# Four small stores of zeros between the first loads of a mixture-of-experts kernel

## The chip, the cores and the metric

The kernel runs on one core of a Trainium2 chip. The metric is the device time of one execution in microseconds, the median of several runs. One further execution is taken by the hardware profiler; all durations below come from that one.

## What is computed

Eight experts each apply a two-layer network to 256 rows of their own. The reference, cut to what matters:

```
x: (8, 256, 512)   w1: (8, 512, 2048)   w2: (8, 2048, 512)   b1: (8, 2048)   b2: (8, 512)   all float32
h   = maximum(x @ w1 + b1, 0)
out = h @ w2 + b2                       (8, 256, 512) float32
```

Each expert has 4 MB of w1 and 4 MB of w2 in memory, so the weights are 64 MB of reads; x adds 4 MB and the output is 4 MB of writes.

## The kernel before

Everything is cast from float32 to float16 while it is loaded: a load issued from GpSimd (POOL in the profile) reads 4 MB of weights and writes 2 MB into the on-chip memory. All weight loads, the x of experts 2 to 7, and the stores of the results of experts 0 to 6 are issued from GpSimd and form one queue, here called the ring. Only the first two x (L188, float32, cast on VectorE at L201), b1 (L189) and the last expert's stores (L142, L143, L149) go by the queues of SyncE and ScalarE.

For an expert e, first_product (L108) computes h transposed: 16 blocks of 128 hidden units, four matmuls each (L113), and ScalarE adds b1, applies the maximum and writes float16 (L120). In the middle of it, the x of the next expert is transposed on TensorE (L100) and copied out by VectorE (L106). second_product (L151) runs three experts later (LAG = 3): b2 is put into the accumulators by a matmul with ones (L163), then 32 matmuls of 128x512 (L175) add h times w2; VectorE and ScalarE copy one half of the rows each (L138, L139), and flush (L130) issues the store (L132).

The order of the ring is written out by hand. The first w1 (L190) and b2 (L191) come first. Then a list of issues, each with the step from which it may go, is built at L221 to L241: for s from 1 on, the x of expert s (load_x, L69), its w1 (load_w1, L75), the w2 of expert s - 3 (load_w2, L85), and from s = 6 on the store of expert s - 6. The w2 of the last expert comes in eight pieces (load_w2_piece, L91), with the remaining stores between them. The main loop (L243) puts the due issues ahead of each step's matmuls. In the text, x2 is the x of expert 2, w1(3) the w1 of expert 3, and so on; the ring begins w1(0), b2, w1(1), x2, w1(2), x3, w1(3), w2(0), x4, w1(4), w2(1), x5, w1(5), w2(2), x6, w1(6), w2(3), store of expert 0, x7, w1(7), w2(4), store of expert 1, w2(5).

An issue waits for its buffer: there are three for w1, three for w2, four for x, three for the results (L42 to L48). It also waits for a completion semaphore: the compiled program gives the transfers of the ring eight of them in turn, so a transfer is not issued before the one eight places ahead of it has landed. For instance, the first x that waits for that, x5, waits for x2, and the store of expert 0 for w1(4).

Of the kernel before, what the change touches and what calls it, by code (L numbers as in the profile page):

```python
# [11 lines left out]
def kernel(  # L12
# [9 lines left out]
    nc = tc.nc  # L22
    fp32 = mybir.dt.float32
# [3 lines left out]
    P = 128  # L27
# [4 lines left out]
    LAG = 3  # L32
# [5 lines left out]
    def ordered(ins):  # L38
        return tc.keep_in_program_order(ins)

    singles = ctx.enter_context(tc.tile_pool(name="singles", bufs=1))
# [14 lines left out]
    b2_sb = singles.tile([1, E * H], fp16)  # L56
    b1_rows = singles.tile([E * 2, M // 2], fp32)
    b1T = singles.tile([P, nJ, E], fp32)

    x16 = [None] * E  # L60
    xT = [None] * E
# [68 lines left out]
    def flush(e):  # L130
        dst, src = pending.pop(e)
        ordered(nc.gpsimd.dma_start(out=dst, in_=src))  # L132

    def store(e, po, c0, c1, split):
        w = c1 - c0
        pool = out_pool if w == H else singles
        out_sb = pool.tile([P, nTB, w], fp32, tag=f"out{c0}_{w}", name=f"out{w}")
        nc.vector.tensor_copy(out=out_sb[:, 0, :], in_=po[0])  # L138
        nc.scalar.copy(out=out_sb[:, 1, :], in_=po[1])  # L139
        dst = out[e].rearrange("(p tb) h -> p tb h", tb=nTB)[:, :, c0:c1]  # L140
        if split and c1 == H:
            nc.sync.dma_start(out=dst[:, 0, :], in_=out_sb[:, 0, :])  # L142
            nc.scalar.dma_start(out=dst[:, 1, :], in_=out_sb[:, 1, :])  # L143
        elif e in RING:
            pending[e] = (dst, out_sb)
        else:
            step = P // PARTS.get(e, 1)
            for lo in range(0, P, step):
                nc.sync.dma_start(out=dst[lo : lo + step], in_=out_sb[lo : lo + step])  # L149

    def second_product(e):  # L151
# [18 lines left out]
        for lo, hi, p0, p1, t in w2_sb[e]:  # L170
            mine = [b for b in blocks if p0 <= b[0] and b[1] <= p1]
            for tb in range(nTB):
                for j in range(lo, hi):
                    for c0, c1, _, _ in mine:
                        ordered(nc.tensor.matmul(  # L175
                            out=acc[c0, tb],
                            lhsT=hT[e][:, j, tb * P : (tb + 1) * P],
                            rhs=t[:, j - lo, c0 - p0 : c1 - p0],
                            start=False,
                            stop=(j == nJ - 1),  # L180
                        ))
            if hi == nJ:
                for c0, c1, _, _ in mine:
                    store(e, [acc[c0, tb] for tb in range(nTB)], c0, c1, e == E - 1)

    x32 = singles.tile([P, nXF32, nTB, H], fp32)
    for e in range(nXF32):
# [4 lines left out]
        out=b2_sb,  # L192
        in_=b2.rearrange("e h -> (e h)").rearrange("(o f) -> o f", o=1),
    ))
    make_identity(nc, ident)
    make_identity(nc, ident16)
    nc.vector.memset(ones1, 1.0)
# [6 lines left out]
    for j in range(nJ):  # L204
        for s in range(2):
            ordered(nc.tensor.matmul(  # L206
                out=pb[s * 64 : (s + 1) * 64, j, :, :],
# [5 lines left out]
    for s in range(2):  # L213
        nc.vector.tensor_copy(  # L214
            out=b1T[s * 64 : (s + 1) * 64, :, :], in_=pb[s * 64 : (s + 1) * 64, :, :, s]
# [4 lines left out]

    ring = []  # L221
    for s in range(1, E + LAG - 1):
        if s < E:
            if s >= nXF32:
                ring.append((s - 2, load_x, (s,)))
            ring.append((s - 2, load_w1, (s,)))
        if s >= LAG:
            ring.append((s - 2, load_w2, (s - LAG,)))
        if s >= 2 * LAG:
            ring.append((s - 2, flush, (s - 2 * LAG,)))  # L230
# [51 lines left out]
```

## Time and profile before

| what | value |
|---|---|
| median of 4 runs | 183.55 us (183.44 to 183.67) |
| the profiled execution, its own time | 183.32 us |
| its span, from the first instruction to the last | 181.5 us |
| TensorE (PE) busy | 137.6 us, 76% of the span |
| ScalarE (ACT) busy | 62.7 us, 35% |
| GpSimd (POOL) busy, issuing transfers for the most part | 22.1 us, 12% |
| VectorE (DVE) busy | 13.4 us, 7% |
| moved by DMA | 40.58 MB counted at the destination, mean 224 GB/s |
| memory read and written | 71.39 MB and 4.19 MB, 416 GB/s over the span |
| one w1 load, issue to landing, median of 8 | 33.7 us |
| one w2 load of 2048 KB, issue to landing, median of 6 | 45.8 us |
| one store of 512 KB from the ring, issue to landing, median of 7 | 27.8 us |

Issue to landing is the time in the queue and in transfer together: the ring is in order, and a load issued early waits there for those ahead of it. A share of the DMA engines can come out a little over 100% in a short window, because a packet is counted where it starts. In lists of instructions, the text in square brackets is the idle time of the engine just before, and what ended it.

### The profile page before, as it was taken

To read this page: it belongs to the slowest core of one execution; us is meant where nothing else is said; L and a number is where in the kernel's file an instruction comes from. 1 tells how busy PE (TensorE), PEld (TensorE's weight loads), DVE (VectorE), ACT (ScalarE), POOL (GpSimd) and SP (SyncE) were. 2 spreads that over 40 slices of the span, in tenths; PEclk is the share of its full clock that TensorE was granted. 3 is DMA by queue.
4 is the path that set the end of the run, shared out by engine and by line. 5 is a ranking of instruction groups with operands and counts; after the bars stand their busy time and mean duration, and the time that the engine had idled before them with its cause. 6 is when DMAs were issued, how large, how long until landed. Compare 5 with 4: busy or idle time off the path is not lost.

```text
span 181.5 us, 2204 instructions
## 1 busy us (share of the span) xinstructions
PE 137.6 (76%) x946; PEld 98.5 (54%) x946; DVE 13.4 (7%) x22; ACT 62.7 (35%) x138; POOL 22.1 (12%) x46
## 2 busy tenths in 40 slices
PE   0555999579650999749992899709999995999890
PEld 0544889469540845637481755707549642434560
DVE  0320011001000101010100101001010010101010
ACT  0022689647660331806063330803409601010100
POOL 7100011300300010111010000200004003113300
PEclk9999999978996699978999699975999999999999
DMA  5989999999999999999998999999999999999995
GB/s 180 279 191 233 231 209 195 207 252 213 197 231 220 199 217 231 192 216 227 231 220 183 232 231 213 191 285 217 199 224 215 283 195 271 217 238 289 214 278 196
DMA packets 7017, 40.58 MB, mean 224 GB/s; under 512 B 1216, under 2 KB 2256, under 8 KB 4960
## 3 DMA queue, kind: packets, MB, share of 16 engines
q0 software_dynamic: 5872, 38.81, 97.9%
q1 hardware_dynamic: 688, 0.95, 1.5%
q10 hardware_dynamic: 448, 0.69, 1.0%
q8 instruction: 7, 0.11, 0.2%
q14 instruction: 2, 0.02, 0.0%
HBM read 71.39 MB, written 4.19 MB: 416 GB/s over the span
## 4 chain that ended last, share of the span: by engine, by line
DMA 70%; PE 14%; issue 8%; another core or an unknown queue 3%; POOL 2%; ACT 0%; POOLq 0%
DMA x<-in_x_dram 24%; DMA w2sb<-in_w_dram 22%; DMA w1sb<-in_w_dram 13%; DMA w<-in_w_dram 11%; PE acc L175 6%; PE ph L113 6%; PE psx L100 1%; POOL w2sb L85 1%; POOL w1sb L75 1%; POOL out_dram L132 0%; PE acc L163 0%; POOL b_sb L191 0%; POOL ident masks.py:199 0%; POOL ident masks.py:197 0%
## 5 line engine op out<-in xcount | busy, mean ns | idle before, releaser
L113 PE MATMUL ph<-xT,w1sb 128*128 128x256 f16 x512 | 68.2, 299 | 8.7 <-DMA w1sb<-in_w_dram 8.7
L120 ACT ACTIVATE hT<-ph,b1T 128x256 f16<-128x256 f32 x128 | 57.0, 474 | 44.0 <-PE ph L113 43.6
L113 PEld LDWEIGHTS <-w1sb 128*128 128x128 f16 x512 | 61.5, 149 | 14.7 <-DMA w1sb<-in_w_dram 9.6
L175 PE MATMUL acc<-w2sb,hT 128*128 128x512 f16 x224 | 49.5, 379 | 1.9 <-DMA w2sb<-in_w_dram 1.9
L175 PEld LDWEIGHTS <-hT 128*128 128x128 f16 x288 | 27.2, 98 | 32.7 <-issue 6.7
L139 ACT COPY out<-acc 128x512 f32<-128x512 f32 (+2 forms) x9 | 4.9, 541 | 59.6 <-PE acc L175 59.6
L100 PE MATMUL psx<-ident,x 128*128 128x128 f16 x64 | 7.0, 275 | 21.1 <-DMA x<-in_x_dram 20.4
L100 PEld LDWEIGHTS <-x 128*128 128x128 f16 x64 | 5.6, 130 | 22.1 <-DMA x<-in_x_dram 21.3
L75 POOL DMA_DIRECT2D w1sb<-in_w_dram x8 | 4.4, 554 | 60.7 <-PE ph L113 59.9
L106 DVE COPY xT<-psx 128x1024 f16<-128x1024 f16 x8 | 5.5, 692 | 83.3 <-PE psx L100 83.3
L138 DVE COPY out<-acc 128x512 f32<-128x512 f32 (+2 forms) x9 | 5.7, 632 | 71.8 <-PE acc L175 71.8
L85 POOL DMA_DIRECT2D w2sb<-in_w_dram x8 | 4.3, 536 | 49.1 <-PE acc L175 49.1
L206 PE MATMUL pb<-ident,b_rows 16*64 16x16 f32 x64 | 3.7, 265 | 6.7 <-DMA b_rows<-in_b_dram 6.7
L175 PE MATMUL acc<-w,hT 128*128 128x320 f16 (+1 forms) x64 | 7.8, 272 | 1.1 <-DMA w<-in_w_dram 1.1
L206 PEld LDWEIGHTS pb<-ident,b_rows 16*64 16x64 f32 x64 | 3.6, 198 | 6.7 <-issue 6.7
L91 POOL DMA_DIRECT2D w<-in_w_dram x8 | 5.0, 624 | 12.0 <-DMA w2sb<-in_w_dram 9.2
L132 POOL DMA_DIRECT2D out_dram<-out x7 | 3.8, 542 | 21.8 <-ACT out L139 13.1
L120 ACT ACT_TABLE_LOAD x1 | 1.3, 1283 | 11.1 <-DVE b1T L214 11.1
L163 PE MATMUL acc<-b_sb,ones 1*128 1x512 f16 (+2 forms) x18 | 4.8, 355 | 0.0
L69 POOL DMA_DIRECT2D x<-in_x_dram x6 | 3.3, 545 | 5.9 <-DMA w2sb<-in_w_dram 5.4
L163 PEld LDWEIGHTS <-ones 1*128 1x128 f16 x18 | 1.1, 92 | 2.2 <-issue 2.1
L201 DVE CAST x<-x 128x1024 f16<-128x1024 f32 x2 | 1.4, 694 | 4.5 <-DMA x<-in_x_dram 4.4
(9 smaller groups left out, 2.6 us busy)
## 6 DMA issues: line engine op xcount, KB each, us to landing
w1sb<-in_w_dram POOLq DMA_DIRECT2D x8, 2048.0 KB, 33.7
w2sb<-in_w_dram POOLq DMA_DIRECT2D x6, 2048.0 KB, 45.8
out_dram<-out POOLq DMA_DIRECT2D x7, 512.0 KB, 27.8
w2sb<-in_w_dram POOLq DMA_DIRECT2D x2, 1024.0 KB, 24.8
x<-in_x_dram POOLq DMA_DIRECT2D x6, 256.0 KB, 38.8
w<-in_w_dram POOLq DMA_DIRECT2D x2, 384.0 KB, 18.9
x<-in_x_dram ACTq DMA_DIRECT2D x1, 512.0 KB, 5.4
x<-in_x_dram SPq DMA_DIRECT2D x1, 512.0 KB, 4.6
```

The lines of the kernel that those rows point to most:

```text
L75: ordered(nc.gpsimd.dma_start(out=w1_sb[e], in_=w1[e].rearrange("(p kc) m -> p kc m", kc=nKC)))
L85: ordered(nc.gpsimd.dma_start(out=t[:, lo : lo + step, :], in_=src[:, lo : lo + step, :]))
L91: ordered(nc.gpsimd.dma_start(out=t, in_=src[:, lo:hi, c0:c1]))
L100: ordered(nc.tensor.transpose(out=pt[:, kc, tb * P : (tb + 1) * P], in_=x16[e][:, tb, :].rearrange("p (q kc) -> p q kc", kc=nKC)[:, :, kc] ...
L106: nc.vector.tensor_copy(out=xT[e], in_=pt)
L113: ordered(nc.tensor.matmul(out=ph, lhsT=w1_sb[e][:, kc, :].rearrange("p (q j) -> p q j", j=nJ)[:, :, j], rhs=xT[e][:, kc, :], start=(kc == 0),
L120: nc.scalar.activation(out=hT[e][:, j, :], in_=ph, func=mybir.ActivationFunctionType.Relu, bias=b1T[:, j, e : e + 1], scale=1.0,)
L138: nc.vector.tensor_copy(out=out_sb[:, 0, :], in_=po[0])
L139: nc.scalar.copy(out=out_sb[:, 1, :], in_=po[1])
L163: ordered(nc.tensor.matmul(out=t, lhsT=ones1, rhs=b2_sb[0:1, e * H + c0 : e * H + c1], start=True, stop=False,))
L175: ordered(nc.tensor.matmul(out=acc[c0, tb], lhsT=hT[e][:, j, tb * P : (tb + 1) * P], rhs=t[:, j - lo, c0 - p0 : c1 - p0], start=False, sto ...
L206: ordered(nc.tensor.matmul(out=pb[s * 64 : (s + 1) * 64, j, :, :], lhsT=b1_rows.rearrange("r (q j) -> r q j", j=nJ)[:, :, j], rhs=ident[0 ...
```

## The change

A tile of 16x128 float32 zeros is made once on VectorE. A new helper, touch(i), stores it from GpSimd to rows 16 i to 16 i + 15 and columns 0 to 127 of expert 0's output. Four of these are put into the ring: touch 0 ahead of x2, touch 1 ahead of x3, touch 2 ahead of x4 and touch 3 ahead of x5. The store of expert 0's result later writes the same rows.

```diff
+    zeros = singles.tile([16, P], fp32)
...
+    def touch(i):
+
+        ordered(nc.gpsimd.dma_start(out=out[0, 16 * i : 16 * (i + 1), 0:P], in_=zeros))
...
+    nc.vector.memset(zeros, 0.0)
     make_identity(nc, ident)
     make_identity(nc, ident16)
...
     ring = []
     for s in range(1, E + LAG - 1):
+        if s > 1 and s < 2 * LAG:
+            ring.append((s - 2, touch, (s - 2,)))
         if s < E:
             if s >= nXF32:
                 ring.append((s - 2, load_x, (s,)))
```

The ring then begins w1(0), b2, w1(1), touch 0, x2, w1(2), touch 1, x3, w1(3), w2(0), touch 2, x4, w1(4), w2(1), touch 3, x5, w1(5), w2(2), x6, and goes on as before. In the compiled program the touches take their turn among the eight completion semaphores. So up to x7 the transfer that an issue waits for is a different one: w2(1) waits for w1(2), x5 for x3, w1(5) for w1(3), w2(2) for w2(0), x6 for touch 2, the store of expert 0 for w2(1) and also for touch 3, x7 for touch 3. The instructions of the other engines are the same in kind, number and order, but for the one memset.

## The prediction

> **What bounds the kernel now.** I read the page from its 40 slices down. The DMA row first, then the queue table, then the chain of work that ended last.
>
> ```profile
> DMA  5989999999999999999998999999999999999995
> ...
> q0 software_dynamic: 5872, 38.81, 97.9%
> ...
> q8 instruction: 7, 0.11, 0.2%
> ...
> DMA 70%; PE 14%; issue 8%; another core or an unknown queue 3%; POOL 2%; ACT 0%; POOLq 0%
> ```
>
> The reader is to see that the 16 DMA engines are 90% busy or more in nearly every slice, that one queue fills them (q0, the GpSimd ring, 97.9% of 16 engines' span), and that DMA makes 70% of the chain. PE is busy for 76% of the span but waits for loads. The other line, q8, is instruction code: 7 packets, 0.2% of 16 x 181.5 us = 5.8 us, so about 0.83 us each on one engine.
>
> The end of the chain in order of time shows the same bound where it counts:
>
> ```profile
> 113.38 39.74 DMA w2sb<-in_w_dram
> 153.11 0.28 issue
> 153.40 19.25 DMA w<-in_w_dram
> 172.65 0.04 issue
> 172.69 3.93 PE acc L175 x32
> 176.62 0.00 issue
> 176.62 0.51 PE acc L175 x4
> 177.13 0.02 issue
> 177.15 0.32 ACT out L139
> ```
>
> From 113.38 to 172.65 us the chain is loads that stand in the ring; PE starts its last 4.44 us when the third piece of the last w2 lands at 172.65, and then come the last stores. So whatever lengthens the work in the ring ahead of 172.65 moves the end by as much, and whatever only moves an issue inside a ring that never runs empty moves nothing.
>
> The third view is the timeline of POOL, where the GpSimd transfers are issued. The nine lines around the places of the four new stores:
>
> ```profile
> 3.29 0.56 POOL L75 DMA_DIRECT2D w1sb<-in_w_dram  x1
> 3.85 0.54 POOL L69 DMA_DIRECT2D x<-in_x_dram  x1
> 4.37 0.55 POOL L75 DMA_DIRECT2D w1sb<-in_w_dram  x1
> 4.89 0.56 POOL L69 DMA_DIRECT2D x<-in_x_dram  x1
> 26.45 0.53 POOL L75 DMA_DIRECT2D w1sb<-in_w_dram  x1 [21.00 <-PE ph L113]
> 26.96 0.55 POOL L85 DMA_DIRECT2D w2sb<-in_w_dram  x1
> 27.48 0.56 POOL L69 DMA_DIRECT2D x<-in_x_dram  x1
> 34.34 0.54 POOL L75 DMA_DIRECT2D w1sb<-in_w_dram  x1 [6.30 <-PE ph L113]
> 34.87 0.55 POOL L85 DMA_DIRECT2D w2sb<-in_w_dram  x1
> ```
>
> An issue takes 0.52 to 0.56 us and POOL idles for 21.00 us before the fourth w1: it is far ahead of the ring.
>
> **The change, part by part.**
>
> The memset of 16x128 zeros on DVE: the memset of ones takes 0.17 us at 0.82, and DVE then idles 4.39 us until x lands at 5.38. Cost 0; without that cover it would be 0.17 us.
>
> Four more issues on POOL, about 0.53 us each. Touch 0 goes at 3.85 and touch 1 two places later, so x2 and w1(2) go 0.53 us later and x3 1.06 us later. Their cover is w1(0) and w1(1), which hold the engines until 15.7 (PE starts at 15.72 on w1(0)) and 26.33 (the chain). Touch 2 follows w2(0) after 27.5, touch 3 follows w2(1); both fall in waits of 6.30 and 11.01 us. Cost 0; bare, it would be 4 x 0.53 = 2.1 us.
>
> The waits. In the compiled order each GpSimd transfer takes one of eight completion semaphores in turn, and waits until the transfer eight places before it has landed. Four more transfers in the window bring that partner nearer, up to x7; behind x7 the pairs are as before. By the landings of before (PE starts on w1(2) at 37.32, on w1(3) at 48.25, on x4 at 59.17, which lands one x load, some 1.25 us, after w2(0), so w2(0) at about 58; POOL's wait for w2(1) ends at 78.81):
> - w2(1) waits for w1(2): issue 34.87 to 37.3. Touch 3 and x5 behind it, for touch 1 and x3: x5 from 35.38 to about 39.
> - w1(5) waits for w1(3): 46.95 to 48.3.
> - w2(2) waits for w2(0): 47.48 to 58, and x6 behind it 48.49 to about 59.
> - w1(6) at 64.71 and w2(3) at 72.26 are held by PE as before (L113 and L175 releasing their buffers), their new partners x4 and w1(4) having landed.
> - The store of expert 0 waits for w2(1), and for touch 3, whose rows it overwrites: 72.88 to 78.8. Behind it x7 goes from 78.81 to 79.4; w1(7) at 85.27 waits for PE as before.
>
> What matters is how much work stands in the ring at the latest of these issues. At 58, w2(0) has just landed and x4, w1(4), w2(1), x5 and w1(5) stand ahead of w2(2). A 4 MB weight takes about (48.25 - 37.32 - 1.25) = 9.7 us, so that is 3 x 9.7 + 2 x 1.25 = 32 us of work. At 37.3, when w2(1) goes out, x3, w1(3), w2(0), x4 and w1(4) stand: 32 us again. Each of the waits delays an issue by 11 us at the most. The ring stays full, and the order of the transfers in it is the same. Cost 0; if the cover went, w2(2)'s delay of 10.5 us would be bare.
>
> The stores' own work in the ring is what remains. Each writes 16 rows of 512 B; with one row to an engine, an engine handles one row and one completion packet. No small store stands in this ring before, so I bound it. Nearest row for a store: ACT's last store, queue q10, in the DMA queue table of the window from 178 to 181.5:
>
> ```profile
> q10 hardware_dynamic: 144, 0.10, 8.5%
> ```
>
> That is 128 rows of 768 B and 16 completions, and 8.5% of 16 x 3.5 us = 4.76 us of engine time, 33 ns a packet. A touch is two packets, 0.066 us on every engine. Nearest row for a 16-row transfer in the ring itself is b2's load, which is queued right behind w1(0). In the DMA issues of the window from 0 to 3 us, the last column being us from issue to landing:
>
> ```profile
> w1sb<-in_w_dram POOLq DMA_DIRECT2D x1, 2048.0 KB, 14.4
> ...
> b_sb<-in_b_dram POOLq DMA_DIRECT2D x1, 8.0 KB, 13.9
> ```
>
> w1(0) is issued at 1.25 and lands at 15.65; b2 is issued at 1.92 and lands at 15.82: 0.17 us later, some of which is latency that the next load hides. So a touch costs between 0.033 us (the completion costing nothing) and 0.17 us, four of them between 0.13 and 0.68. I take 0.066, since it comes from a store of nearly this row length: 4 x 0.066 = **0.26 us**. A gain is not excluded by any row, but nothing is taken out of the ring either.
>
> Could a store to memory hold an engine until its data has landed? The rows speak against it: expert 0's 512 KB store lands at 72.88 + 48.6 = 121.48 (the longest of that line), and x7, next in the ring, lets PE start at 122.75, 1.27 us later; x6, which follows a load (w2(2), landed at 99.13 where POOL's wait ends), lets PE start at 100.44, 1.31 us later. The load behind a store is no slower than the load behind a load.
>
> The Trainium skill has a rule that speaks against the change: "DMA: Bandwidth & Descriptors", section "Anatomy of one DMA — SWDGE (gpsimd) path", gives about 2.0 us fixed for a DMA, most of it the receipt of the write, heaviest to HBM. If that time were held in the ring, four stores would cost an estimated 8 us; b2's 0.17 us and the pair 1.27 and 1.31 us say that in a full ring it is latency beside other work, so the measurement decides.
>
> **Sum.** 0 + 0 + 0 + 0.26 us. The profiled execution took 183.32 us with a span of 181.5, so it would take 183.58. It lies 0.23 below the median of the runs; the median of 183.55 goes to **183.8 us**, +0.14%. About 0.2% (0.37 us) is what a measurement of this kernel can tell from no change, so this counts as the same.
>
> **Rivals.**
>
> *The small stores stall the ring (slower).* Mechanism: a store's completion waits for its write to land, and the engine's next packet stands behind it. Place: each of the 16 engines, four times, all before 80 us, on the chain. It decides from 0.37 / 4 = 0.09 us per touch. At b2's 0.17 us it gives 0.68 us, 184.2 us; if the 2.8 us that the last store (L143) needs from issue to landing were held each time, 11 us, 194.8. For it: b2's landing, and that no row here has a small store between loads. Against it: the pair of x loads above. Chance 0.34, nearly all of it near the lower price.
>
> *The engines come out more level (faster).* A load lands when the slowest of 16 engines is done, and seven code packets of 0.83 us each fall on single engines. If the shifted moments put one less on the engine that sets the end, 0.83 - 0.26 = 0.57 us is gained: 183.0 us. For it: such a packet is three times the whole cost of the touches. Against it: PE's instructions, and so its fetches, are the same ones in the same order. The same dice could add 0.83 us. Chance 0.12.
>
> *The ring runs dry (slower).* If fewer transfers in flight left it empty once at w2(2), up to 10.5 us, 194. The 32 us of queued work speak against it. Chance 0.02, within the slower side.
>
> *It does nothing that can be seen.* The touches' packets could slip into gaps between other packets: 183.55. The range of the forecast includes that.
>
> **How the numbers follow.** Forecast, within 0.2%: 0.52. Slower by over 0.2%: 0.34 + 0.02 = 0.36. Faster: 0.12. Range 183.3 to 184.6: from a quarter microsecond below the median (a small part of the levelling) over b2's price (184.2) to that price with half a code packet on top (0.42); it leaves out about 0.1 on either side.
>
> **What would show it.** Right: w2(2) issued near 58 and expert 0's store near 78.8 on POOL, DMA digits of 9 in the slices from 26 to 90 us, PE's start on x4 later by about 0.2 us (three touches), on x5 and on the piece that ended at 172.65 by about 0.26. The rival of the stall: the delay grows in steps of 0.17 us or more at each touch. Dry ring: a digit below 9 near 58 or 90 us. Levelling: landings after 90 us earlier than before although those by 60 us are later. Wrong altogether if the rows of a touch go to few engines instead of sixteen: then 16 x 0.033 = 0.53 us would fall on one engine each time, 2.1 us if always the same.

## The result, and the profile after

| kernel | median | runs | ratio to before, 95% interval |
|---|---|---|---|
| before | 183.50 us (183.09 to 184.16) | 57 | |
| with the four stores | 183.76 us (183.47 to 184.08) | 39 | 1.0012 (1.0007 to 1.0016) |

The ratio is +0.22 us, with an interval of 0.13 to 0.29. The profiled execution took 183.52 us (183.32 before), its span is 181.7 us (181.5 before).

The page of the changed kernel, the rows that answer to those of before: the DMA engines in 40 slices, the ring's queue, the code queue, the shares of the chain.

```profile
DMA  5989999999999899999998999999899999999995
...
q0 software_dynamic: 6000, 38.84, 97.9%
...
q8 instruction: 7, 0.11, 0.2%
...
DMA 80%; PE 8%; issue 8%; POOL 1%; ACT 0%; POOLq 0%
```

The queue has 128 packets more: four times 16 rows and 16 completions. DMA still bounds the kernel, and the code packets are the same seven. There is a new digit 8 at the 14th slice (59 to 64 us) and one at the 29th, but it means nothing: in the stretch from 59 to 64 both kernels have a DMA share of 1.01 and 216 GB/s, and a kernel with no touch in the ring, only their tile (e3 below), shows seven digits of 8, where the kernel before has two:

```profile
DMA  5989998999899989998999899999899999999994
```

The end of the chain in order of time, start and length in us:

```profile
113.49 39.53 DMA w2sb<-in_w_dram
153.03 0.28 issue
153.31 19.36 DMA w<-in_w_dram
172.67 0.04 issue
172.71 3.93 PE acc L180 x32
...
177.19 0.32 ACT out L144
```

This is the surprise. The piece that PE waits for ends at 172.67, and at 172.65 before: 0.02 us later, not 0.26. The last copy starts at 177.19 (177.15 before). Yet the span is 0.18 us longer (181.52 and 181.70). One pair of landings proves little, since profiles of one and the same ring (before, and e0 and e3 below) put the end of this piece between 172.65 and 172.93. But in this pair most of the added time lies behind the last line of the chain, in a stretch of 4 us that I had not opened.

That stretch is found under the line that opens the program (L277 before, L285 after), to which the closing instructions belong. One row of it in each kernel: engine, operation, count, shortest, median and longest in ns, first and last start in us. Before:

```profile
L277 POOLq DRAIN  x3: 51/107/9406, 171.3 to 181.2; - x3
```

After:

```profile
L285 POOLq DRAIN  x3: 46/98/9557, 171.4 to 181.4; - x3
```

GpSimd's first DRAIN starts with the issue of the last store of the ring (171.33 us before, 171.37 after) and takes 9.406 us before and 9.557 after. The closing barrier waits for it last: SyncE, the next to be done, is ready 0.09 us ahead of its end before and 0.26 after. The store itself lands 7.8 us after its issue in both kernels (the shortest figure of the stores' time to landing, L132 and L133):

```profile
DMA to landing us min/median/max: 7.8/27.8/43.6
```

So GpSimd goes on for 1.60 us after its last transfer has landed before the change, and for 1.77 after it. The last store of all, by ScalarE's or SyncE's queue, lands at 180.50 and 180.52; GpSimd's DRAIN ends at 180.73 and 180.93, and the program 0.79 and 0.78 us after that. From here on this DRAIN is called the drain.

### The profile page after: what moved, and what is told of

Its sections match the earlier page's. It is cut to its first block, busy times and chain, and to the rows that moved or that the text cites. A ratio compares the mean times of both kernels' runs of the same rounds, so it can differ in the third digit from the quotient of the medians.

```text
span 181.7 us, 2211 instructions
## 1 busy us (share of the span) xinstructions
PE 137.8 (76%) x946; PEld 98.6 (54%) x946; DVE 13.4 (7%) x23; ACT 62.7 (35%) x138; POOL 24.3 (13%) x50
## 4 chain that ended last, share of the span: by engine, by line
DMA 80%; PE 8%; issue 8%; POOL 1%; ACT 0%; POOLq 0%
DMA w2sb<-in_w_dram 39%; DMA x<-in_x_dram 23%; DMA w<-in_w_dram 11%; DMA w1sb<-in_w_dram 8%; PE ph L114 5%; PE acc L180 2%; POOL w1sb L76 0%; POOL w2sb L86 0%; PE psx L101 0%; ACT out L144 0%; POOLq L86 0%; POOLq L274 0%; POOLq L133 0%
## 5 line engine op out<-in xcount | busy, mean ns | idle before, releaser
L133 POOL DMA_DIRECT2D out_dram<-out x7 | 3.8, 542 | 28.1 <-ACT out L144 13.1
L137 POOL DMA_DIRECT2D out_dram<-zeros x4 | 2.0, 508 | 0.0
```

## The experiments

All times in us. Theory 1 is that of the prediction (packets in the ring). Theory 2 (the packets hide, the end of the program is later) came from comparing the two profiles, theory 3 is the rival of the dry ring, and theory 4, the drain, was formed after the first four runs. The change in us is the ratio to the kernel before, taken times 183.5.

| kernel | change (95%) | transfers in the ring | last of them landed | drain ended | difference | per transfer |
|---|---|---|---|---|---|---|
| before | | 38 | 179.13 | 180.73 | 1.60 | 0.042 |
| after | +0.22 (0.13 to 0.29) | 42 | 179.16 | 180.93 | 1.77 | 0.042 |
| e0 before again | -0.04 (-0.18 to 0.13) | 38 | 179.21 | 180.81 | 1.60 | 0.042 |
| e1 four again | +0.29 (0.13 to 0.46) | 42 | 179.26 | 181.03 | 1.77 | 0.042 |
| e2 twelve | +0.64 (0.42 to 0.88) | 50 | 179.62 | 181.71 | 2.09 | 0.042 |
| e3 memset only | +0.02 (-0.15 to 0.18) | 38 | 179.44 | 181.03 | 1.60 | 0.042 |
| e4 twelve by SyncE | +0.35 (0.18 to 0.50) | 38 | 179.29 | 180.89 | 1.60 | 0.042 |
| e5 w1 in halves | +1.14 (0.86 to 1.39) | 46 | 179.77 | 181.69 | 1.93 | 0.042 |
| e6 four results not stored | 178.79, one run | 34 | 173.81 | 175.25 | 1.43 | 0.042 |
| e7 twelve loads | +0.77 (0.50 to 1.05) | 50 | 179.37 | 181.46 | 2.09 | 0.042 |
| e8 late store | +1.16 (0.94 to 1.39) | 38 | 179.21 | 180.81 | 1.60 | 0.042 |
| e9 late store, twelve | +1.45 (1.19 to 1.71) | 50 | 180.06 | 182.15 | 2.09 | 0.042 |
| e10 one store of 64 rows | +0.11 (-0.04 to 0.28) | 39 | 179.45 | 181.09 | 1.64 | 0.042 |

The landings are the last completion events of the ring in the trace. Profiles of kernels with one and the same ring put the last landing between 179.13 and 179.44 (before, e0, e3), so a single landing does not show a tenth of a microsecond; the difference to the drain's end does, since it repeats to 0.01. In the nine profiles in which the drain is done after SyncE, the program ends 0.78 to 0.79 us after the drain; in the other four (e4, e6, e8, e9) SyncE is done later, and it is 1.03 to 2.11 us.

**e0 and e1: both kernels once more.**

> The kernel before, once more, as a measure of what this chip and a second profile change by themselves. Both theories: ratio 1.000 within 0.1%, span 181.5 us within 0.2. In the profiled pair the change added 0.18 us to the span, of which only 0.02 stood at the landing of the last store (180.50 to 180.52 us) and some 0.16 between it and the end of the program. If the ring holds the cost (theory 1), that tail of 1.0 us will differ from profile to profile of one and the same kernel; if the end of the program holds it (theory 2), the tail here is again the shorter one.

> The changed kernel, once more. Both theories: +0.15 to +0.3 us. Theory 1 (each store adds a row packet and a completion packet on every engine of the full ring): landings behind the touches later by 0.1 to 0.3 us than in the repeated kernel before. Theory 2 (the packets hide; the end of the program is later): landings later by under 0.1 us, and the last 1.0 us of the program longer by 0.16 us again.

The repeats agree with the first pair. From the landing of the last store to the end of the program it is 1.03 us in both profiles of the kernel before and 1.19 and 1.18 in those of the changed one. The closing landings ahead of it move by under 0.1 (172.72 to 172.77, and 180.57 to 180.63). In the middle, PE's start on x7 is 0.25 us later (122.63 and 122.88), but without any touch it lies anywhere from 122.63 to 123.04 (before, e0, e3). That is theory 2: 0.16 of the change lies at the end.

**e2: three touches in each place.**

```diff
-        ordered(nc.gpsimd.dma_start(out=out[0, 16 * i : 16 * (i + 1), 0:P], in_=zeros))
+        for k in range(3 * i, 3 * i + 3):
+            ordered(nc.gpsimd.dma_start(out=out[0, 16 * k : 16 * (k + 1), 0:P], in_=zeros))
```

> Three touches of different rows at each of the four places, twelve in all; 16 rows each as before. Theory 1, 0.05 to 0.066 us each: +0.6 to +0.8 us over the kernel before. Theory 2: no more than with four, +0.2 us, since small packets hide and the end of the program is as before. If the waits on the eight completion semaphores mattered (theory 3), several microseconds, since twelve more transfers in the window hold the sixth w1 and the fourth w2 back by a further 14 and 7 us and the ring holds only 11 to 22 us of work at its lowest instead of 32.

+0.64: the number of theory 1, and theory 2 in the form "no more than four cost" is gone. But the profile puts it in the place of theory 2. The end of the program takes 1.54 us behind the last store's landing instead of 1.03, and the drain is the longer one:

```profile
L285 POOLq DRAIN  x3: 46/98/9904, 171.8 to 182.2; - x3
```

4 more transfers lengthen the drain by 0.17, 12 more by 0.49, and 38, 42 and 50 transfers times 0.042 us give its whole length after the last landing. This is theory 4. The waits did not matter: several microseconds would have shown.

**e3: the tile and its memset alone.**

```diff
-    def touch(i):
-
-        ordered(nc.gpsimd.dma_start(out=out[0, 16 * i : 16 * (i + 1), 0:P], in_=zeros))
...
-        if s > 1 and s < 2 * LAG:
-            ring.append((s - 2, touch, (s - 2,)))
```

> The tile of zeros and its memset alone, no touch. Theory 1: 0.00 us, below what can be told. Theory 2 in the form that the shifted layout of the on-chip memory or the memset makes the difference: +0.2 us; in the form that four more GpSimd instructions make the end of the program later: 0.00.

+0.02 (-0.15 to 0.18): neither the memset nor the tile of zeros costs anything that can be seen.

**e4: twelve stores of the same rows and size by another queue.** They come later than the touches, with the transposes, and store values of x.

```diff
+                if e < 4:
+                    touch(e)
...
+        nc.vector.tensor_copy(out=zeros[:, i, :], in_=xT[i + 1][0:16, 0, 0:P])
+        for k in range(3 * i, 3 * i + 3):
+            nc.sync.dma_start(out=out[0, 16 * k : 16 * (k + 1), 0:P], in_=zeros[:, i, :])
```

> Twelve stores of the same rows and size, but issued from SyncE by its own queue, three each after the copy of the transposed x of experts 1 to 4 (they store 16x128 values of that x, which the result overwrites). The GpSimd ring has its 38 transfers again. Theory 1 (packets on the engines): the same 12 rows and completions on every engine, so +0.5 to +0.7 us as with twelve in the ring. Theory 4 (GpSimd's last drain instruction ends 0.042 us times the number of transfers in the ring after the last of them has landed: 1.60 us with 38, 1.77 with 42, 2.09 with 50 so far): the drain ends 1.60 us after the last landing, the last 1.0 us of the program are as before, and the whole gains only what the packets cost, +0.05 to +0.25 us.

The drain is back at 1.60 us, as theory 4 has it, with the same 192 rows on the engines:

```profile
L285 POOLq DRAIN  x3: 51/108/9372, 171.5 to 181.6; - x3
```

The whole is +0.35, more than the 0.25 at which I had put the upper end. The profile tells why: the program ends 1.29 us behind the last landing, not 1.03, though the drain is short. At its end SyncE checks the completion semaphores one by one, 0.06 us each; in the kernel before most of these checks are done while the last stores are under way, and here, with SyncE's semaphores handed round by the twelve stores, two of the last stores' stand at the front of the list, so six more checks follow that of the last landing, and SyncE is done after the drain. It is 0.26 at SyncE in place of the drain's 0.49, and about 0.1 for the packets.

**e5: more transfers without a touch.**

```diff
-        ordered(nc.gpsimd.dma_start(
-            out=w1_sb[e], in_=w1[e].rearrange("(p kc) m -> p kc m", kc=nKC)
-        ))
+        src = w1[e].rearrange("(p kc) m -> p kc m", kc=nKC)
+        for lo in (0, 64):
+            ordered(nc.gpsimd.dma_start(out=w1_sb[e][lo : lo + 64], in_=src[lo : lo + 64]))
```

> No touches; every w1 load is cut in two of 64 partitions each, with the same rows, so that the ring has 46 transfers instead of 38. Theory 4: the drain ends 46 x 0.042 = 1.93 us after the last landing, +0.34 us at the end of the program, and with eight more completions on every engine (8 x 0.022 = 0.18 at most) +0.35 to +0.55 us in all. Theory 1: 8 completions x 0.033 = +0.26 us in the ring and an unchanged end. If the lengthening belongs to stores to memory alone, the end of the program is as before.

The drain does what theory 4 says, 1.93 us for 46 transfers, so it is not about stores. Nor does it go by packets: this ring has 6000, as many as the changed kernel's, whose drain takes 1.77. The whole, +1.14, is outside both expectations: 0.33 of it is the drain, and some 0.8 arises in the ring. The completions explain more of that than the 0.18 expected: by their packet records they take 1.05 us on each engine, 0.75 before, so 0.30. What a load of 64 partitions costs beyond that was not pursued.

**e6: fewer transfers.** The results of experts 0 to 3 are not stored.

```diff
-        ordered(nc.gpsimd.dma_start(out=dst, in_=src))
+        if e > 3:
+            ordered(nc.gpsimd.dma_start(out=dst, in_=src))
```

> The stores of experts 0 to 3 are left out (their rows of the output are not written), so that the ring has 34 transfers. The whole falls by about 4 x 1.3 = 5.2 us, the time of these stores on the engines. Theory 4: GpSimd's drain ends 34 x 0.042 = 1.43 us after the last ring transfer has landed. Theory 1 has no reason for another figure than the 1.60 us of the kernel before.

The drain ends 1.43 us after the last landing, 34 x 0.042, as theory 4 has it in this direction too. The one run is 4.65 us shorter than the kernel before beside it (183.44), where 5.2 was expected. Here the drain sets the end no longer: it is done at 175.25, SyncE at 175.72.

**e7: loads in place of the stores.** The edit is against the kernel before.

```diff
+    zeros = singles.tile([16, 12, P], fp32)
...
+    def touch(i):
+        for k in range(3 * i, 3 * i + 3):
+            ordered(nc.gpsimd.dma_start(out=zeros[:, k, :], in_=x[0, 16 * k : 16 * (k + 1), 0:P]))
...
+        if s > 1 and s < 2 * LAG:
+            ring.append((s - 2, touch, (s - 2,)))
```

> Twelve loads of 16 rows of 512 B (from x, into a tile that nobody reads) at the places of the twelve stores. Theory 4: the drain ends 50 x 0.042 = 2.10 us after the last landing, and the whole is +0.5 to +0.75 us, as with twelve stores. If the cost lay in the write to memory and its receipt (the rival of the stall): under +0.3 us.

+0.77 (0.50 to 1.05) beside +0.64 with stores, and the same drain:

```profile
L284 POOLq DRAIN  x3: 51/97/9917, 171.5 to 182.0; - x3
```

A small load costs no less than a small store, so the write to memory and its receipt are not the price.

**e8 and e9: the drain under cover.** A late store makes SyncE end the program; e9 adds the twelve touches.

```diff
             nc.sync.dma_start(out=dst[:, 0, :], in_=out_sb[:, 0, :])
+            nc.sync.dma_start(out=dst[0:16, 0, :], in_=out_sb[0:16, 0, :])
```

> The kernel before, and behind SyncE's last store a further one that writes 16 of its rows again; it is issued only when the store ahead has landed (180.5 us), and lands some 2 us later. So SyncE ends the program, at about +2 us, and GpSimd's drain (180.73 us) ends under cover. Of interest as the base of the next kernel.

> The same late store, and twelve touches in the ring as in e2. The drain ends at about 181.7 us again (2.09 us after the last ring landing), but now ahead of the late store's landing. Theory 4 (0.042 us a transfer at the drain, little in the ring): over e8 only what the ring costs, +0.10 to +0.25 us, instead of the +0.64 of e2. Theory 1 (the cost is in the ring): over e8 the same +0.6 us as without the late store.

The late store lands 1.4 us after the one ahead of it, not 2, so that e8 is +1.16 and not about +2, and it covers the drain in both: in e9 the drain ends at 182.15 and SyncE only after 182.82, the landing. With the cover the end of the program is no longer (0.93 and 0.92 us behind the last landing), so 0.5 of the price of twelve touches should be gone. The ratios differ by 0.0016, 0.29 us instead of 0.64, but the difference of two intervals reaches from -0.06 to 0.64, and the medians (184.71 and 185.15) differ by 0.44. Both lie between the 0.25 of theory 4 and the 0.6 of theory 1, so this pair does not settle it. What carries theory 4 is the drain's length in all the profiles, and the 0.78 to 0.79 us from its end to that of the program wherever SyncE is done first.

**e10: one store of 64 rows for the four.**

```diff
-    zeros = singles.tile([16, P], fp32)
+    zeros = singles.tile([64, P], fp32)
...
-        ordered(nc.gpsimd.dma_start(out=out[0, 16 * i : 16 * (i + 1), 0:P], in_=zeros))
+        ordered(nc.gpsimd.dma_start(out=out[0, 0:64, 0:P], in_=zeros))
...
-        if s > 1 and s < 2 * LAG:
+        if s == 2:
```

> One store of 64 rows ahead of x2 in place of the four of 16 rows: the same bytes and row packets, one completion and one transfer instead of four. Theory 4: the drain ends 39 x 0.042 = 1.64 us after the last landing, and the whole is +0.04 for the drain and up to 0.06 for the ring, +0.04 to +0.10 us. Theory 1: four rows and a completion an engine, 5 x 0.033 = +0.17 us, all in the ring.

The drain takes 1.64 us, as theory 4 has it for 39 transfers. The whole, +0.11 (-0.04 to 0.28), can't tell 0.07 from 0.17; its middle lies between them.

## Why the prediction was right, and where it was not

**The number was right, the place was not.** Forecast +0.26 us, all in the ring; measured +0.22 (0.13 to 0.29), of which the drain and so the end of the program has 0.16 to 0.17 (four transfers at 0.042 each) and the rest of the program about 0.05 (-0.04 to 0.13). That the two sum to nearly the forecast is a coincidence of 0.066 us a touch in the ring, as I had it, and 0.042 at the end plus some 0.013 in the ring, as it is.

**The step that failed** is the cost of 0 for "Four more issues on POOL". The prediction asked only whether they delay the ring, and let nothing but the ring ahead of 172.65 move the end: behind the chain's last line, 177.15 us, it has "and then come the last stores" and no term. Between that line and 181.5 lie the last stores, GpSimd's drain and the closing barrier, and the drain, not a store, is what comes last; each of the four issues lengthens it by 0.042 us. No line of the page names it, but the rows of the program's first line did: a DRAIN of 9406 ns that begins where the last store is issued.

**The term that was mis-sized** is 0.066 us a touch in the ring. Twelve touches cost 0.64 us in all and 0.49 at the drain, which leaves 0.15 (-0.07 to 0.39) for the ring, 0.012 each; twelve loads leave 0.28 (0.01 to 0.56), 0.023 each, and e9 over e8 gives 0.024 to 0.037 each. In the profiled pair PE's start on x4, three touches on, is 59.24 for 59.17, and on x5 79.86 for 79.80, where I had said 0.2 and 0.26; but without any touch these starts lie between 58.97 and 59.47, and between 79.66 and 80.09. The duration itself was too high as well: in the touches' own records a row takes 40 ns and a completion 9, 0.05 us for the two, and where three touches stand in a row (e2) 0.04 on average. That makes 0.20 us for four and 0.49 for twelve, both above what the intervals leave to the ring (0.13 and 0.39), so here a packet's duration was not its price; the loads and e9 do not exclude that it was. Why small packets should cost less than they last was not tried.

**The waits on completion semaphores went as worked out, and cost nothing.** The issues on POOL in the changed kernel:

```profile
37.55 0.53 POOL L86 DMA_DIRECT2D w2sb<-in_w_dram  x1 [2.71 <-DMA w1sb<-in_w_dram]
38.07 0.50 POOL L137 DMA_DIRECT2D out_dram<-zeros  x1
39.50 0.55 POOL L70 DMA_DIRECT2D x<-in_x_dram  x1 [0.93 <-DMA x<-in_x_dram]
48.77 0.53 POOL L76 DMA_DIRECT2D w1sb<-in_w_dram  x1 [8.71 <-DMA w1sb<-in_w_dram]
58.16 0.53 POOL L86 DMA_DIRECT2D w2sb<-in_w_dram  x1 [8.87 <-DMA w2sb<-in_w_dram]
58.68 0.54 POOL L70 DMA_DIRECT2D x<-in_x_dram  x1
64.83 0.53 POOL L76 DMA_DIRECT2D w1sb<-in_w_dram  x1 [5.61 <-PE ph L114]
72.37 0.53 POOL L86 DMA_DIRECT2D w2sb<-in_w_dram  x1 [7.02 <-PE acc L180]
79.33 0.54 POOL L133 DMA_DIRECT2D out_dram<-out  x1 [6.43 <-DMA out_dram<-zeros]
79.85 0.53 POOL L70 DMA_DIRECT2D x<-in_x_dram  x1
85.38 0.53 POOL L76 DMA_DIRECT2D w1sb<-in_w_dram  x1 [4.99 <-PE ph L114]
```

Worked out were 37.3, about 39 (x5), 48.3, 58, 59, 64.71, 78.8, 79.4 and 85.27. The brackets name the new partners: w1 and w2 landings where PE had been, and touch 3 ahead of the store of expert 0. Issues that went up to 10.7 us later changed nothing, since the ring had some 30 us of work standing by the working of the prediction; in e2 they went later still, and no lost time shows there either.

**The memset**: nothing, as said (e3).

**The rivals.** The stall of the ring by a store's write: no, four touches leave it 0.05, and loads cost no less (e7); at b2's 0.17 us a touch it would have been 0.68. Its point of decision, 0.09 us a touch, lies above the measured total of 0.055. The levelling of the engines: no gain in either pair of profiles. The dry ring: no. A sign that I named for it, a digit below 9 near 58 us, was a bad one, since a kernel without touches shows as many (e3).

## What to carry to other kernels

The chain of work ends before the program does. Open the closing instructions as well, under the line that starts the program: which of them the last barrier waits for, and whether its length depends on something that the change adds. Here each transfer issued from GpSimd costs 0.042 us there, whatever its size and however early it was issued, as long as the drain ends last; so merging small transfers (e10, a drain of 1.64 us for 1.77) or keeping them off that queue (e4, 1.60) shortens it. The gain ends where another engine is done last: in the kernel before, SyncE is done only 0.09 us before the drain, about two transfers, and in e4 and e6 it is SyncE that ends last. Where in the queue the transfers stand was not tried.

A right total is not a right account: a count of packets and a count of transfers gave the same number here, and only a dose of three, another queue and the split of the profile into its stretches told them apart.

## What the runs showed of the hardware that was not expected

- GpSimd's closing DRAIN ends 0.042 us times the number of transfers it has issued after the last of them has landed: 1.43, 1.60, 1.64, 1.77, 1.93 and 2.09 us for 34, 38, 39, 42, 46 and 50 transfers, loads or stores, in 13 profiles.
- SyncE's closing checks of completion semaphores take 0.06 us each and go in a fixed order; in e4 that order made the end 0.26 us longer.
- A 16-row transfer between large loads of a full ring costs some 0.01 to 0.04 us of the ring's time (0.03 at most by the intervals for four and twelve stores, 0.05 for twelve loads); its two packets last 0.04 to 0.05 us, and those of a store by another queue lasted 0.066.
- Cutting the eight w1 loads at partition 64 cost about 0.8 us beyond the drain, 0.30 of it in longer and more completion packets; the cause of the rest is open.
